# Who splits u while tiles are routed, when selections are transposed, and how many odd columns are made early in a PEER layer

## The chip, the cores and the metric

The kernel runs on one core of a Trainium2 chip. The metric is the device time of one execution in microseconds (us); several runs are given by their median. Engines carry the profile's names: PE is TensorE (matmuls), PEld its weight loads, DVE is VectorE, ACT is ScalarE, POOL is GpSimd, SP is SyncE, whose queue issues nearly all loads and stores.

## The reference, cut to what matters

The program computes two blocks on 512 tokens of width 1024; the change touches only the last layer of the second, an expert layer (PEER) with 16384 experts:

```python
def block(xb):                                   # xb: tokens x 1024
    q = (xb @ w_query).reshape(T, 8, 2, 128)     # 8 heads, 2 halves
    s = einsum('thpk,hpnk->thpn', q, sub_keys)   # 128 keys per half
    top_s, top_i = lax.top_k(s, 16)
    cand_s = top_s[:, :, 0, :, None] + top_s[:, :, 1, None, :]
    cand_i = top_i[:, :, 0, :, None] * 128 + top_i[:, :, 1, None, :]
    best_s, best_pos = lax.top_k(cand_s.reshape(T, 8, 256), 16)
    idx = take_along_axis(cand_i.reshape(T, 8, 256), best_pos, -1)
    gate = jax.nn.softmax(best_s, axis=-1)
    u, v = expert_u[idx], expert_v[idx]
    act = jax.nn.gelu(einsum('td,thkd->thk', xb, u))
    return einsum('thk,thkd->td', gate * act, v)
...
x = x + gate2 * peer(h, ...)
return rmsnorm(x, final_norm_w)
```

## The kernel before

A float32 product is made of three matmuls (`mm3`, L203): each operand is a rounded high part and a rest, and al x bh, ah x bl and ah x bh are added. The tokens are split once (`hh`, `hl`, L288, L289). A weight comes as a **unit** of 128 x 1024 values: `unit` (L190) loads 512 KB into a `raw` buffer (3 of them) through SyncE's queue, and `split` (L194) has ScalarE write `whi` (L201) and another engine the rest `wlo` (L202), VectorE unless `eng` names another. There are 8 buffers each for `whi` and `wlo`, so a unit can be split when TensorE has used the one eight before it.

The first 128 tokens take the reference's way: their selected rows of u and v are gathered by GpSimd (L1075). For the other 384 tokens the layer is computed densely. The experts are 128 columns of 128. For column j, `expert_in` (L1057) multiplies a unit of u with the tokens: 8 x 3 matmuls of 384 columns, then Gelu on ScalarE (L1063); this is called a unit of TensorE here. The 64 even columns are made early and stored in memory (`actD`), and the odd ones are made in the last stage.

`peer` runs two generators step by step. `route` first makes the queries in 16 steps (`w_q` units, L1104 onwards, with searches of the 16 best on VectorE, `top16`). Then it routes four tiles of 128 tokens, all on VectorE: candidates (`cand`, L1112), the best 16 of 256 per head, and the indices by comparing and reducing (`eq` L1137, product L1139, `si` L1142), then the softmax (`g`). `selected` (L1160) transposes `si0`, `si1` and `g` of a tile by TensorE (L1167) and copies them to `sel` on ScalarE. `gates_dense` (L1181) then makes, for 12 chunks of 32 tokens, the matrix of gates over all experts: rows `ga` and `gb` by VectorE (L1207, L1211, L1214), ScalarE or GpSimd (L1200), one matmul per token (L1217), a copy to `gst` (L1219), and four stores to memory (`gD`, L1224). Between the steps, `pace` says how many units of u are issued: its pairs are (steps, units), and they sum to 64.

`experts_out` (L1228) is the last stage. `parts(j)` (L1244) loads the gates of eight columns (`gt`, L1248), takes or makes the column's activations, multiplies them with the gates (L1258), splits the result into `wh` and `wl` (L1262, L1263), and loads and splits the unit of v. `prod` then accumulates 3 x 2 x 3 matmuls of 512 columns per column. Odd columns in `early` are made ahead of the loop:

```python
early = {j: self.expert_in(T, psp.only("pre"), j, nc.vector) for j in (1, 3, 5)}
...
ready = [parts(j) for j in range(AHEAD)]           # AHEAD = 2
```

What is written in this order is not what runs: a scheduler with a timeline of its own (`schedule_with_timeline_sim`) chooses each engine's order of instructions ahead of time, with the pools' buffers as limits. Each engine then runs its own list in order.

Of the kernel before, what the change touches and what calls it, by code (L numbers as in the profile page):

```python
# [172 lines left out]
class Block:  # L173
# [850 lines left out]
    def peer(self):  # L1024
        tc, nc, a = self.tc, self.nc, self.a
        dt = slice(128, S)
        n = S - 128
        with ExitStack() as c0:
            dr = c0.enter_context(tc.tile_pool(name="pdr", bufs=1, space=DRAM))
            self.actD = dr.tile([NSPILL, 128, n], F32, name="actD")  # L1030
            self.gD = dr.tile([12, 128, 4096], F32, name="gD")
            P = c0.enter_context(tc.tile_pool(name="pe", bufs=1, reuse_waits="tile"))
            self.acc0 = P.tile([128, D], F32, name="acc0")
            self.eid = P.tile([128, 128], I32, name="eid")
            self.gate0 = P.tile([128, 128], F32, name="gate0")
            with ExitStack() as c1:
                Q = c1.enter_context(tc.tile_pool(name="pra", bufs=1, reuse_waits="tile"))
                psp = _Banks(self.psum, t=[6, 7], u=[4, 5, 0], g=[1, 2, 3])
                sel = [Q.tile([128, NT - 1, 128], F32, name=f"sel{i}") for i in range(3)]
                iota = self.const(Q, "iota")  # L1040
                pace = [(1, 3), (15, 10), (32, 37), (24, 14)]
                self.pend = []
                work = [self.route(Q, psp, sel, iota), self.gates_dense(psp, sel, iota)]
                j, self.gpool = 0, None
                for steps, us in pace:
                    for i in range(steps):
                        _advance(work)
                        for _ in range((i + 1) * us // steps - i * us // steps):
                            act = self.expert_in(self.gpool or Q, psp, 2 * j, nc.gpsimd, "ga" if self.gpool else "act")
                            nc.sync.dma_start(self.actD[j], act)  # L1050
                            j += 1
                assert j == NSPILL
                while work:
                    _advance(work)
            self.experts_out()

    def expert_in(self, pool, psp, j, eng, tag="act"):  # L1057
        n = S - 128
        w = self.unit(self.a["p_u"][j], eng=eng)
        ps = psp.tile([128, S], F32, name="u")[:, :n]  # L1060
        self.proj_t(ps, w, self.hh, self.hl, slice(128, S))
        act = pool.tile([128, S], F32, name=tag, bufs=6)[:, :n] if tag == "ga" else pool.tile([128, n], F32, name=tag, bufs=4)
        self.nc.scalar.activation(act, ps, AF.Gelu)  # L1063
        return act

# [23 lines left out]
    def route(self, Q, psp, sel, iota):  # L1089
        tc, nc, a = self.tc, self.nc, self.a  # L1090
        with tc.tile_pool(name="rt", bufs=1, reuse_waits="tile") as R:
            sk = R.tile([128, 16, 128], F32, name="sk")
            nc.sync.dma_start(sk, a["skT"].rearrange("p (m n) -> p m n", m=16))
            val = R.tile([128, NT, 16, 16], F32, name="val")
            idx = R.tile([128, NT, 16, 16], U32, name="idx")
            for m in range(16):
                w = self.unit(a["w_q"][m])
                ps = psp.tile([128, S], F32, name="t")
                self.proj_t(ps, w, self.hh, self.hl)
                q = R.tile([128, S], F32, name="q", bufs=2)  # L1100
                nc.scalar.activation(q, ps, AF.Copy)
                ps = psp.tile([128, NT, 128], F32, name="t")
                for t in range(NT):
                    nc.tensor.matmul(ps[:, t, :], q[:, 128 * t:128 * t + 128], sk[:, m, :], start=True, stop=True)  # L1104
                sc = R.tile([128, NT, 128], F32, name="sc", bufs=2)
                nc.scalar.activation(sc, ps, AF.Copy)
                for t in range(NT):
                    self.top16(R, sc[:, t, :], val[:, t, m, :], idx[:, t, m, :])
                yield
            for t in range(NT):  # L1110
                cand = R.tile([128, 8, 16, 16], F32, name="cand")
                nc.vector.tensor_tensor(cand, val[:, t, 0::2, :, None].to_broadcast([128, 8, 16, 16]),  # L1112
                                        val[:, t, 1::2, None, :].to_broadcast([128, 8, 16, 16]), op=ALU.add)
                fi = R.tile([128, 16, 16], F32, name="fi")
                nc.vector.tensor_copy(fi, idx[:, t])
                best = R.tile([128, 8, 16], F32, name="best")
                pos = R.tile([128, 8, 16], U32, name="pos")
                yield
                for h in range(8):
                    self.top16(R, cand[:, h].rearrange("p a b -> p (a b)"), best[:, h, :], pos[:, h, :])  # L1120
                    if h == 3:
                        self.selected(psp, sel)
                    if h % 2:
                        yield
                ab = R.tile([128, 2, 8, 16], U32, name="ab")
                nc.vector.tensor_scalar(ab[:, 0], pos, 4, None, op0=ALU.logical_shift_right)
                nc.vector.tensor_scalar(ab[:, 1], pos, 15, None, op0=ALU.bitwise_and)
                abf = R.tile([128, 2, 8, 16], F32, name="abf")
                nc.vector.tensor_copy(abf, ab)
                tok = []  # L1130
                for i in range(2):
                    eq = R.tile([128, 8, 16, 16], F32, name="eq")
                    for h in range(0, 8, 4):
                        hs = slice(h, h + 4)
                        io = iota[:, None, :16].to_broadcast([128, 64, 16])
                        ab_ = abf[:, i, hs].rearrange("p h k -> p (h k)")[:, :, None].to_broadcast([128, 64, 16])
                        nc.vector.tensor_tensor(eq[:, hs].rearrange("p h k a -> p (h k) a"), ab_, io,  # L1137
                                                op=ALU.is_equal)
                    nc.vector.tensor_tensor(eq, eq, fi[:, i::2, None, :].to_broadcast([128, 8, 16, 16]),  # L1139
                                            op=ALU.mult)  # L1140
                    r = Q.tile([128, 8, 16], F32, name=f"si{i}", bufs=2)
                    nc.vector.tensor_reduce(r, eq, AX.X, ALU.add)  # L1142
                    tok.append(r)
                    yield
                g = Q.tile([128, 8, 16], F32, name="g", bufs=2)
                gs = R.tile([128, 8], F32, name="gs")
                nc.vector.tensor_tensor(g, best, best[:, :, 0:1].to_broadcast([128, 8, 16]), op=ALU.subtract)
                nc.scalar.activation(g, g, AF.Exp)
                nc.vector.tensor_reduce(gs, g, AX.X, ALU.add)
                nc.vector.reciprocal(gs, gs)  # L1150
                nc.vector.tensor_tensor(g, g, gs[:, :, None].to_broadcast([128, 8, 16]), op=ALU.mult)
                tok.append(g)
                if t == 0:
                    nc.vector.scalar_tensor_tensor(self.eid, tok[1].rearrange("p h k -> p (h k)"), 128.0,
                                                   tok[0].rearrange("p h k -> p (h k)"), op0=ALU.mult, op1=ALU.add)
                    nc.vector.tensor_copy(self.gate0, g.rearrange("p h k -> p (h k)"))
                else:
                    self.pend.append((t, [v.rearrange("p h k -> p (h k)") for v in tok]))
                yield
# [67 lines left out]
    def experts_out(self):  # L1227
# [5 lines left out]
        with ExitStack() as c0:  # L1233
# [3 lines left out]
            T = c0.enter_context(tc.tile_pool(name="eow", bufs=2, reuse_waits="tile"))  # L1237
            psp = _Banks(self.psum, u=[4, 5], pre=[0, 1, 2], acc=[0, 1, 2, 3, 6, 7])
            g2 = self.gate_row(P, psp.only("u"), 40, "g2")
            early = {j: self.expert_in(T, psp.only("pre"), j, nc.vector) for j in (1, 3, 5)}  # L1240
            acc = [[psp.tile([128, 512], F32, name="acc") for h in range(2)] for t in range(NT - 1)]
            gts = {}

            def parts(j):  # L1244
# [3 lines left out]
                    nc.sync.dma_start(gts[g].rearrange("p c j t -> p c (j t)"),  # L1248
                                      self.gD[:, :, 256 * g:256 * g + 256].rearrange("c i n -> i c n"))
                if j % 2 == 0:  # L1250
                    act = T.tile([128, n], F32, name="acts", bufs=3)
                    nc.sync.dma_start(act, self.actD[j // 2])
                elif j in early:
                    act = early.pop(j)
                else:
                    act = self.expert_in(T, psp, j, nc.vector)
                v = self.unit(a["p_v"][j])
                nc.vector.tensor_tensor(act.rearrange("p (c t) -> p c t", t=32), act.rearrange("p (c t) -> p c t", t=32),  # L1258
                                        gts[g][:, :, jj, :], op=ALU.mult)
# [107 lines left out]
```

## Time and profile before

| | us |
|---|---|
| median of 3 runs | 2299.18 (2296.61 to 2304.81) |
| profiled execution, its own time | 2295.14 |
| its span in the trace | 2293.4 |
| PE busy in the span | 2202.0 (96%) |
| DVE busy | 1653.9 (72%) |
| ACT busy | 921.4 (40%) |
| POOL busy | 817.0 (36%) |

Times of the trace count from the span's start. The queries of the layer end at about 1163 us, the tiles are routed until about 1321, the gates are made until 1472, the first product of the last stage starts at 1502, and the last matmul of the loop is near 2277. Busy shares are means over stages; what a stage waits for is read from the stretch itself. A row of the timeline gives start, duration, engine, line, operation, tiles (out<-in) and form; in square brackets stands the idle time of the engine before it and what released it.

### The profile page before, as it was taken

What the parts mean: (1) busy time and instruction counts of PE and PEld (TensorE: products, weight loads), DVE (VectorE), ACT (ScalarE), POOL (GpSimd) and SP (SyncE); (2) the same over time, 40 slices, a digit from 0 to 9 for tenths busy, and PEclk for the clock granted to TensorE, in tenths of its full rate; (3) what the DMA queues carried; (4) which work ended last, traced back from release to release, by engine and by line L of the source; (5) the groups of instructions that cost most, each with busy time, mean ns of one, the idle gap of its engine ahead of it and who ended that gap; (6) DMA issues with size and microseconds to landing.
All of it is one profiled execution on the core that took longest, in us unless ns stands there. A gap on an engine that the chain in (4) does not pass through costs nothing. (4 is left out here: it accounts for less than half of the span.)

```text
span 2293.4 us, 32152 instructions
## 1 busy us (share of the span) xinstructions
PE 2202.0 (96%) x11849; PEld 1953.9 (85%) x11849; DVE 1653.9 (72%) x3073; ACT 921.4 (40%) x1540; POOL 817.0 (36%) x611
## 2 busy tenths in 40 slices
PE   7898999999999999999998989989999999999997
PEld 6686878888889888889998989968888888888886
DVE  4346657888526478556589999678888787888888
ACT  4215544333325443343343467633333333333332
POOL 3133210000002223231456688634444443444445
PEclk9999999999999999999999999999999999999999
DMA  7423105767332321053345456799999989999996
GB/s 247 125 63 97 38 1 194 234 220 234 104 99 79 101 83 56 10 175 118 118 138 162 149 182 241 283 339 343 339 336 347 352 334 343 327 345 338 348 334 212
DMA packets 165646, 469.53 MB, mean 205 GB/s; under 512 B 18801, under 2 KB 62705, under 8 KB 165361
## 3 DMA queue, kind: packets, MB, share of 16 engines
q1 hardware_dynamic: 128624, 333.25, 42.7%
q0 software_dynamic: 36864, 134.23, 16.0%
q8 instruction: 93, 1.52, 0.3%
q14 instruction: 65, 0.52, 0.1%
HBM read 422.31 MB, written 39.85 MB: 202 GB/s over the span
## 5 line engine op out<-in xcount | busy, mean ns | idle before, releaser
L207 PE MATMUL b<-hh,wlo 128*128 128x384 f32 (+2 forms) x1872 | 657.3, 352 | 8.3 <-DVE wlo L202 2.8
L208 PE MATMUL b<-hl,whi 128*128 128x384 f32 (+2 forms) x1872 | 655.1, 350 | 3.6 <-DVE hl L289 3.4
L209 PE MATMUL b<-hh,whi 128*128 128x384 f32 (+2 forms) x1872 | 654.3, 350 | 0.0
L201 ACT ACTIVATE whi<-raw 128x1024 fp32r<-128x1024 f32 (+1 forms) x405 | 425.3, 1055 | 372.4 <-PE b L209 171.5
L202 DVE TENSOR_TENSOR wlo<-raw,whi 128x1024 fp32r<-128x1024 f32 (+1 forms) x326 | 397.7, 1228 | 201.9 <-ACT whi L201 196.6
L202 POOL TENSOR_TENSOR wlo<-raw,whi 128x1024 fp32r<-128x1024 f32 x79 | 209.2, 2661 | 527.0 <-ACT whi L201 520.4
L207 PEld LDWEIGHTS b<-hh,wlo 128*128 128x128 f32 x1872 | 354.7, 190 | 36.8 <-issue 4.3
L208 PEld LDWEIGHTS b<-hl,whi 128*128 128x128 f32 x1872 | 355.8, 190 | 30.6 <-DVE hl L289 3.8
L209 PEld LDWEIGHTS b<-hh,whi 128*128 128x128 f32 x1872 | 355.8, 190 | 25.3 <-issue 0.4
L207 PE MATMUL b<-whi,wl 128*128 128x512 f32 x768 | 299.6, 390 | 11.3 <-DVE wl L1263 11.3
L209 PE MATMUL b<-whi,wh 128*128 128x512 f32 x768 | 300.5, 391 | 0.0
L208 PE MATMUL b<-wlo,wh 128*128 128x512 f32 x768 | 300.4, 391 | 0.0
L1075 POOL DMA_INDIRECT grow<-in_p_ur_dram,eid x128 | 171.4, 1339 | 244.1 <-DVE gact L1078 170.8
L1075 POOL DMA_INDIRECT grow<-in_p_v_dram,eid x128 | 173.2, 1353 | 213.4 <-DVE acc L1080 126.7
L1063 ACT ACTIVATE act<-b 128x384 f32<-128x384 f32 x114 | 55.6, 490 | 356.1 <-PE b L209 313.5
L207 PE MATMUL b<-whi,hl 128*128 128x512 f32 (+1 forms) x464 | 179.5, 388 | 4.6 <-DVE hl L255 2.4
L207 PEld LDWEIGHTS b<-whi,wl 128*128 128x128 f32 x768 | 144.6, 188 | 40.4 <-DVE wl L1263 11.6
L209 PE MATMUL b<-whi,hh 128*128 128x512 f32 (+1 forms) x464 | 178.4, 385 | 0.0
L208 PE MATMUL b<-wlo,hh 128*128 128x512 f32 (+1 forms) x464 | 178.2, 384 | 0.0
L209 PEld LDWEIGHTS b<-whi,wh 128*128 128x128 f32 x768 | 144.5, 188 | 30.3
L208 PEld LDWEIGHTS b<-wlo,wh 128*128 128x128 f32 x768 | 144.5, 188 | 28.9
L1080 DVE SCALAR_TENSOR_TENSOR acc<-grow,gact,acc 128x1024 f32<-128x1024 f32 x127 | 162.5, 1280 | 5.8 <-DMA grow<-in_p_v_dram,eid 4.7
(296 smaller groups left out, 2972.5 us busy)
## 6 DMA issues: line engine op xcount, KB each, us to landing
raw<-in_p_u_dram SPq DMA_DIRECT2D x128, 512.0 KB, 4.5
raw<-in_p_v_dram SPq DMA_DIRECT2D x128, 512.0 KB, 6.7
raw<-in_w_adaT_dram SPq DMA_DIRECT2D x48, 512.0 KB, 3.8
gD<-gst SPq DMA_DIRECT2D x48, 512.0 KB, 4.5
gt<-gD SPq DMA_DIRECT2D x16, 1536.0 KB, 12.5
raw<-in_w_up_dram SPq DMA_DIRECT2D x44, 512.0 KB, 4.3
raw<-in_w_t_dram SPq DMA_DIRECT2D x32, 512.0 KB, 3.6
acts<-actD SPq DMA_DIRECT2D x64, 192.0 KB, 5.6
```

Of the source, the lines that this page charges most:

```text
L201: nc.scalar.activation(hi, raw, AF.Copy)
L202: (eng or nc.vector).tensor_tensor(lo, raw, hi.bitcast(F32), op=ALU.subtract)
L207: mm(out, al, bh, start=start, stop=False)
L208: mm(out, ah, bl, start=False, stop=False)
L209: mm(out, ah, bh, start=False, stop=stop)
L1063: self.nc.scalar.activation(act, ps, AF.Gelu)
L1075: nc.gpsimd.indirect_dma_start(out=g, out_offset=None, in_=rows[n], in_offset=bass.IndirectOffsetOnAxis(ap=self.eid[:, s:s + 1], axis=0))
L1080: nc.vector.scalar_tensor_tensor(self.acc0, g, act[:, s:s + 1], self.acc0, op0=ALU.mult, op1=ALU.add)
```

## The change

Three things are changed. The splits of u in the first and the third part of `pace` (37 of 64) go from GpSimd to VectorE, and three units move from the third part to the fourth. The transposes of a tile's selections are written behind the second product of the next tile instead of behind its fourth search. Five odd columns instead of three are made ahead of the last stage; for these `act` gets 6 buffers in place of 4, and `acts` 2 in place of 3.

```diff
-                pace = [(1, 3), (15, 10), (32, 37), (24, 14)]
+                pace = [(1, 3), (15, 10), (32, 34), (24, 17)]
...
-                for steps, us in pace:
+                for n_, (steps, us) in enumerate(pace):
...
-                            act = self.expert_in(self.gpool or Q, psp, 2 * j, nc.gpsimd, "ga" if self.gpool else "act")
+                            act = self.expert_in(self.gpool or Q, psp, 2 * j, nc.vector if n_ in (0, 2) else nc.gpsimd,
+                                                 "ga" if self.gpool else "act")
...
-    def expert_in(self, pool, psp, j, eng, tag="act"):
+    def expert_in(self, pool, psp, j, eng, tag="act", nact=4):
...
-        act = pool.tile([128, S], F32, name=tag, bufs=6)[:, :n] if tag == "ga" else pool.tile([128, n], F32, name=tag, bufs=4)
+        act = pool.tile([128, S], F32, name=tag, bufs=6)[:, :n] if tag == "ga" else pool.tile([128, n], F32, name=tag, bufs=nact)
...
-                    if h == 3:
-                        self.selected(psp, sel)
...
+                    if i:
+                        self.selected(psp, sel)
...
-            early = {j: self.expert_in(T, psp.only("pre"), j, nc.vector) for j in (1, 3, 5)}
+            early = {j: self.expert_in(T, psp.only("pre"), j, nc.vector, nact=6) for j in (1, 3, 5, 7, 9)}
...
-                    act = T.tile([128, n], F32, name="acts", bufs=3)
+                    act = T.tile([128, n], F32, name="acts", bufs=2)
...
-                    act = self.expert_in(T, psp, j, nc.vector)
+                    act = self.expert_in(T, psp, j, nc.vector, nact=6)
```

The scheduler makes new lists from this. Behind `L1050` the line numbers differ by one or two between the kernels. In these lists a name's number tells tiles of one name apart, and an operand without number is one of its tiles.

VectorE, second half of the routing of tile 0, before: comparisons (`eq`), products, reductions (`si`) and searches of the next tile follow each other.

```order
L1142 TENSOR_REDUCE si_9949<-eq 128x128
L1156 COPY gate_8234<-g 128x128
L1177 MATCH_REPLACE rest<-best,cand 128x256 x2
L1137 TENSOR_TENSOR eq<-abf,c_iota 128x1024 x2
L1178 MAX best<-rest 128x8 x2
L1139 TENSOR_TENSOR eq<-eq,fi 128x2048
L1179 MAX_INDEX pos<-best,rest 128x8 x2
L1142 TENSOR_REDUCE si_9989<-eq 128x128
```

The same place after:

```order
L1143 TENSOR_REDUCE si_9949<-eq 128x128
L1178 MATCH_REPLACE rest<-best,cand 128x256 x2
L202 TENSOR_TENSOR wlo<-raw,whi 128x1024
L1136 TENSOR_TENSOR eq<-abf,c_iota 128x1024 x2
L1179 MAX best<-rest 128x8 x2
L202 TENSOR_TENSOR wlo<-raw,whi 128x1024
L1138 TENSOR_TENSOR eq<-eq,fi 128x2048
L1180 MAX_INDEX pos<-best,rest 128x8 x2
L202 TENSOR_TENSOR wlo<-raw,whi 128x1024
L1143 TENSOR_REDUCE si_9989<-eq 128x128
```

Three splits stand between two reductions here, where none stood; in the whole route there are 21.

TensorE, the first matmuls of the gates (`b` is a bank of results), before:

```order
L207 MATMUL b_11576<-hh,wlo 128x384
L208 MATMUL b_11576<-hl,whi 128x384
L209 MATMUL b_11576<-hh,whi 128x384
L1217 MATMUL b_11324<-gb,ga 128x128 x4
L1217 MATMUL b_11306<-gb,ga 128x128 x4
L1217 MATMUL b_11337<-gb,ga 128x128 x4
L207 MATMUL b_11576<-hh,wlo 128x384
```

The same place after:

```order
L209 MATMUL b_11576<-hh,whi 128x384
L1168 MATMUL b_11082<-c_ident,si_10685 128x128
L1168 MATMUL b_11082<-c_ident,si_10732 128x128
L1168 MATMUL b_11082<-c_ident,g 128x128
L1168 MATMUL b_11506<-c_ident,si_11042 128x128
L1168 MATMUL b_11506<-c_ident,si_11089 128x128
L1168 MATMUL b_11506<-c_ident,g 128x128
L1218 MATMUL b_11222<-gb,ga 128x128 x4
L1218 MATMUL b_11204<-gb,ga 128x128 x4
```

The transposes of tiles 2 and 3 now stand directly ahead of the first gate matmul. Before, those of tile 2 stood among the units ahead of it, and those of tile 3 behind it.

VectorE, from the last rows of gates to the first products with `gt`, before:

```order
L1211 TENSOR_SCALAR ga_13143<-c_iota_8241,sel0_8238,sel2_8240 128x128 x4
L202 TENSOR_TENSOR wlo_13463<-raw_13460,whi_13462 128x1024
L202 TENSOR_TENSOR wlo_13500<-raw_13497,whi_13499 128x1024
L202 TENSOR_TENSOR wlo_13535<-raw_13532,whi_13534 128x1024
L1078 ISA grow_13199,gact_13198<-grow_13199,h2_6035 128x1024
L1078 ISA gact_13198 128x1
L1258 TENSOR_TENSOR act_13249<-act_13249,gt_13325 128x384
```

The same place after:

```order
L1215 TENSOR_TENSOR gb_13144<-c_iota_8241,sel1_8239 128x512
L202 TENSOR_TENSOR wlo_13422<-raw_13419,whi_13421 128x1024
L202 TENSOR_TENSOR wlo_13457<-raw_13454,whi_13456 128x1024
L202 TENSOR_TENSOR wlo_13494<-raw_13491,whi_13493 128x1024
L202 TENSOR_TENSOR wlo_13529<-raw_13526,whi_13528 128x1024
L1259 TENSOR_TENSOR act_13249<-act_13249,gt_13391 128x384
```

Four splits instead of three stand ahead of the first product with `gt`, and the gather's product (L1078) has moved behind it.

## Rows read from the trace of the kernel before

**Rows 1.** Busy time by stretch: us, PE, PEld, DVE, ACT, POOL busy (instructions), PEclk, DMA share, GB/s.

```profile
1163.00:1328.00 165.00, 147.25 (x823) 145.64 (x821) 163.91 (x367) 65.41 (x96) 106.94 (x39) 0.96 0.52 153
1328.00:1472.00 144.00, 143.84 (x1102) 143.77 (x1102) 138.19 (x360) 109.95 (x235) 120.20 (x98) 0.99 0.62 231
1472.00:1505.00 33.00, 18.89 (x88) 17.61 (x88) 14.19 (x22) 9.19 (x15) 5.78 (x6) 0.80 0.98 351
1505.00:2277.00 772.00, 772.00 (x3728) 680.32 (x3727) 630.71 (x814) 270.48 (x372) 338.52 (x250) 1.00 0.92 335
```

**Rows 2.** Waits of TensorE over the program: total us, times, longest us.

```profile
PE b L207 <- DVE wl L1263: 11.3, 1, 11.3
...
PE b L1217 <- DVE gb L1214: 6.9, 1, 6.9
...
PE b L208 <- DVE hl L289: 3.4, 2, 2.9
```

**Rows 3.** Timeline, VectorE then TensorE, ends of the route: start us, us, instruction [idle before].

```profile
1166.96 3.58 DVE L1112 TENSOR_TENSOR cand<-val 128x2048 f32<-128x2048 f32 x1
...
1321.30 5.18 DVE L1207 TENSOR_SCALAR gb<-c_iota,sel,sel 128x128 f32<-128x128 f32 x4
...
1330.26 0.86 DVE L1207 TENSOR_SCALAR gb<-c_iota,sel,sel 128x128 f32<-128x128 f32 x3
...
1328.16 1.22 PE L1217 MATMUL b<-gb,ga 128*128 128x128 f32 x4 [6.92 <-DVE gb L1214]
```

**Rows 4.** Groups by form, 1167 to 1321.3 us, VectorE then GpSimd: busy us, mean ns.

```profile
L1137 DVE TENSOR_TENSOR eq<-abf,c_iota 128x1024 f32<-128x1024 f32 x16 | 31.9, 2035 | 0.0
L1139 DVE TENSOR_TENSOR eq<-eq,fi 128x2048 f32<-128x2048 f32 x8 | 21.9, 2732 | 0.0
...
L1112 DVE TENSOR_TENSOR cand<-val 128x2048 f32<-128x2048 f32 x4 | 11.6, 2894 | 0.0
...
L1115 DVE CAST fi<-idx 128x256 f32<-128x256 uint32 x4 | 2.9, 722 | 0.0
...
L1151 DVE TENSOR_TENSOR g<-g,gs 128x128 f32<-128x128 f32 x4 | 2.5, 619 | 0.0
...
L1147 DVE TENSOR_TENSOR g<-best 128x128 f32<-128x128 f32 x4 | 2.5, 618 | 0.0
...
L1156 DVE COPY gate<-g 128x128 f32<-128x128 f32 x1 | 1.8, 1789 | 0.0
...
L202 POOL TENSOR_TENSOR wlo<-raw,whi 128x1024 fp32r<-128x1024 f32 x33 | 97.1, 2957 | 55.9 <-ACT whi L201 55.9
```

**Rows 5.** Timeline, VectorE then GpSimd: four single operations of the route and of a split.

```profile
1223.72 0.28 DVE L1115 CAST fi<-idx 128x256 f32<-128x256 uint32 x1
...
1227.80 2.27 DVE L1112 TENSOR_TENSOR cand<-val 128x2048 f32<-128x2048 f32 x1
...
1236.63 2.34 DVE L1137 TENSOR_TENSOR eq<-abf,c_iota 128x1024 f32<-128x1024 f32 x2
...
1299.27 2.40 POOL L202 TENSOR_TENSOR wlo<-raw,whi 128x1024 fp32r<-128x1024 f32 x1 [2.07 <-ACT whi L201]
```

**Rows 6.** Timeline of the hole: VectorE, then SyncE, then TensorE.

```profile
1474.57 1.30 DVE L202 TENSOR_TENSOR wlo<-raw,whi 128x1024 fp32r<-128x1024 f32 x1 [6.44 <-ACT whi L201]
1478.73 1.23 DVE L202 TENSOR_TENSOR wlo<-raw,whi 128x1024 fp32r<-128x1024 f32 x1 [2.86 <-ACT whi L201]
1483.27 1.23 DVE L202 TENSOR_TENSOR wlo<-raw,whi 128x1024 fp32r<-128x1024 f32 x1 [3.31 <-ACT whi L201]
1484.41 1.22 DVE L1078 CUSTOM_DVE_ANT_0 grow<-grow,h 128x1024 f32<-128x1024 f32 x1
...
1495.70 1.50 DVE L1258 TENSOR_TENSOR act<-act,gt 128x384 f32<-128x384 f32 x3 [10.07 <-DMA gt<-gD]
...
1482.02 0.49 SPq L1248 DMA_DIRECT2D gt<-gD  x1
...
1501.87 0.79 PE L207 MATMUL b<-whi,wl 128*128 128x512 f32 x1 [11.32 <-DVE wl L1263]
```

## The prediction

> **What bounds the kernel now.** I read the stretches first. In the last stage (1505 to 2277 us) TensorE is busy 772.00 us of 772.00, and in the gate stage (1328 to 1472 us) 143.84 of 144.00 [rows 1]. There only work taken off TensorE shortens the time. Time without work is left in two places that the change touches. While tiles are routed (1163 to 1328 us) TensorE works 147.25 us of 165.00 and VectorE 163.91: VectorE sets the end. In the hole before the first product (1472 to 1505 us) TensorE works 18.89 of 33.00 at a granted clock of 0.80, with the DMA engines at 0.98 [rows 1]. The list of waits then says who ends the idle time: 11.3 us at the first product for the weights of v's gates (L1263), 6.9 us at the first gate matmul for gb (L1214), and 2.9 us at most for hl when the stage starts [rows 2].
>
> VectorE's route runs without a gap from the first cand at 1166.96 to the first gate rows at 1321.30, which is 154.3 us; the first gate matmul starts at 1328.16 [rows 3]. Part of this is not VectorE's own work. Its two-operand operations take longer while GpSimd splits: the sixteen eq take 31.9 us, the eight products 21.9, the four cand 11.6, and small copies up to 1.8 each, beside 33 splits on GpSimd [rows 4]. Undisturbed, a pair of eq takes 2.34, a cand or a product (both 2048 wide) 2.27, a small copy 0.28 [rows 5]. The excess is 31.9 - 8 x 2.34 = 13.2; 21.9 - 8 x 2.27 = 3.7; 11.6 - 4 x 2.27 = 2.5; and 1.8 + 1.4 + 1.4 + 1.5 for the four small groups: 25.5 us, or 0.78 per split of GpSimd. Searches with one operand show none.
>
> **The change, part by part.** All sums are against the profiled execution's 2295.14 us.
>
> *Splits on VectorE.* Of the units of u, 37 get their subtraction from VectorE. In VectorE's order 21 stand between the first cand and the last reduction of the route, and one more just ahead of it. A split on VectorE delays the next instruction by 1.14 us (1483.27 to 1484.41) [rows 6], so this adds 21 x 1.14 = 23.9, and 1.14 ahead of it. It removes the 33 splits of GpSimd from that stretch and with them the 25.5. So this half of the change is near to nothing: VectorE pays in work what it paid in waiting. But the third segment ends before the route does. GpSimd's order holds 11 splits of the fourth segment that start as soon as a buffer is freed, and these fall beside the second half of the route. At the rate above they cost 11 x 0.78 = 8.6. Nearest bounds: nothing, if they meet one-operand searches; and the whole length of an undisturbed split, 2.40 [rows 5], each: 26.4. I take the rate because it is a mean over 33 of them in the same program. I add 2.3 (0 to 6) for the first gate rows that GpSimd builds in the same stretch and for splits that wait for whi. Behind the route VectorE's first four gate rows no longer meet GpSimd: 5.18 us before, while three of the same alone take 0.86 [rows 3], so four 1.1: -4.1. When the stage starts, three splits go to VectorE ahead of hl: between -2.9 (the wait is gone [rows 2]) and +3.4 (three splits in front); I take +1.0.
>
> *Selections a tile later.* Before, tile 3's transposes stood behind the first gate matmuls in TensorE's order. Now tile 2's and tile 3's six transposes all stand ahead of the first one. So short waits become one long one. TensorE has 32.4 units ahead of the first gate matmul (before 33.9). A unit takes 4.16 us of TensorE, as the splits at 1474.57 and 1478.73 show, each released by the end of one unit [rows 6]. 32.4 x 4.16 = 134.8 from 1163: it is done at about 1298, and then waits for VectorE some 35 us. The first gate matmul is VectorE's to give, and all terms so far move it one for one: 1.0 + 1.1 - 25.5 + 23.9 + 8.6 + 2.3 - 4.1 = **+7.3 us**, to about 1335.5.
>
> *Work carried into the gate stage.* Between the first and the last gate matmul TensorE now has 338 matmuls of units, before 314, and three transposes fewer: 24 x 4.16 / 24 = 4.2, less an estimated 0.4 for the transposes (the 128 wide matmuls at 0.1 each): **+3.8**. Nothing hides it, since this stage has no idle time.
>
> *Five odd columns.* After the last gate matmul TensorE had 3 units and 7 matmuls ahead of the first product, 13.7 us; now it has 4 units and 22 matmuls, 20.5 us. The product itself hangs on the last gates' way through memory: the load of gt is issued at 1482.02, about 10 us after the last gate matmul (1472, where the stretch of [rows 1] ends), lands by 1495.70, and the product starts at 1501.87 [rows 6]. In the new order SyncE's queue has one raw load ahead of gt instead of two, but four splits of VectorE precede its first product with gt instead of three. I take this chain as 29.6 us against 29.9: **-0.3**. So the added 6.8 us lie in the hole's idle time, and one unit less is left for the last stage: **-4.2**. That is the one sure gain. Two more columns made early do not mean two units less, since one of the two moves work that already stood ahead of the first product. The act and acts buffers change nothing that a row shows: cost nothing, while loads land before use.
>
> Sum: 7.3 + 3.8 - 0.3 - 4.2 = **+6.6**. 2295.14 + 6.6 = 2301.7 own time. The median of the runs is 2299.18, 4.0 above the profiled execution, so **2305.7**. A measurement can tell about 0.3%, 6.9 us, from no change, so this lies at the very bound.
>
> **A rule against the change.** The rows show VectorE's pair of eq at 2.34 undisturbed and at 31.9/8 = 4.0 in the mean beside GpSimd [rows 4, 5]. The Trainium skill, "SBUF — State Buffer", section "Who interferes with whom", says that VectorE's second port and GpSimd's are one shared pair, held as an exclusive lock. By that rule in its strict form every split left on GpSimd would shut out the route's two-operand work for its whole length, which is the third case below. The rate of 0.78 of 2.40 agrees with the lock for a third of the time, about the share of such operations in the route (46 of 129 us undisturbed).
>
> **Rivals.** *The late splits fall into gaps.* The 11 meet searches and the start gains: then 8.6 and 2.3 fall away, the start gives up to -2.9, and if gt also lands some us earlier, since fewer loads share the queue, the hole's remaining 9 us shrink. Sum: from 6.6 - 8.6 - 2.3 - 3.9 = -8, and to -14 with gt, up to +2. For it: the new route's waits for whi could pull the two apart. Against it: GpSimd starts whenever a buffer comes free, and two-operand work is over a third of VectorE's time. It ends faster than before where the 11 cost under 0.18 us each. This is the case on the other side.
> *Each late split blocks for its whole length.* 11 x 2.4 in place of 8.6: up to +24, from +13. For it: the worst pair of eq are far above the mean. Against it: 33 splits cost 25.5 together, not 79.
> *The hole is not shortened.* If gt is late by the 4.2 us, or the unit made early is paid by a later hole, the last term is gone: about +11. For it: DMA share 0.98 there [rows 1]. Against it: the chain starts from the last gate matmul as before.
>
> **Chances.** Forecast (+2 to +13) 0.55: of it 0.29 within 6.9 us and 0.26 slower. Late splits in gaps 0.24: 0.12 faster, 0.12 within. Full blocking 0.13 and no shorter hole 0.08, both slower. So faster 0.12, the same 0.41, slower 0.47. Range: from -5 to +18.5 about the median, 2294 to 2318, which leaves out the lower part of the first rival and the top of the second. The forecast's own range is 2301 to 2312.
>
> **What would show it.** In the new trace: VectorE without idle time until about 1333; pairs of eq at 2.34 until the fourth segment's splits begin on GpSimd near 1256, and longer ones behind that; in the list of waits one wait of some 35 us of TensorE ahead of the first gate matmul in place of several short ones; the first gate matmul near 1335.5 and the last near 1483; idle time of about 9 us before the first product near 1513; and 768 us to the tail with TensorE always busy. I am wrong if eq stays long although GpSimd is quiet (then it is not GpSimd that stretches it), if the first gate matmul comes before 1328, or if TensorE shows idle time in the last stage.

## The result, and the profile after

The changed kernel takes **2319.27 us** (median of 6 runs, 2316.48 to 2320.29), the kernel before 2296.70 beside it (6 runs): a ratio of 1.0092, 95% interval 1.0074 to 1.0109. On the scale of the prediction, whose median before was 2299.18, that is 2320.3: slower, as forecast, but by 21 us and not by 6.6, and just above the range's top of 2318 (the two medians themselves are 22.6 apart). Its profiled execution has a span of 2315.8 us, 22.4 more than before.

Where the 22.4 us lie is read best by cutting both traces at the same five events: the last matmul of the scores, the first and the last matmul of the gates, the first product (the first L207 of `whi` and `wl` behind them), and TensorE's last matmul.

| us, from the traces | before | after | difference | forecast |
|---|---|---|---|---|
| to the last scores | 1163.0 | 1165.2 | +2.2 | +1.0 |
| to the first gate matmul | 165.2 | 169.4 | +4.2 | +6.3 |
| gates, first to last matmul | 144.1 | 153.7 | +9.6 | +3.8 |
| hole, to the first product | 29.6 | 27.8 | -1.8 | -0.3 |
| last stage, to TensorE's last matmul | 777.7 | 773.5 | -4.2 | -4.2 |
| tail, to the end | 13.8 | 26.2 | +12.4 | 0 |

The first difference is not the change's alone: the scores end at 1161.8 us in one and at 1174.8 in another of the kernels below (e1, e2). The stretches of the changed kernel between these events, with the columns of [rows 1]:

```profile
1165.20:1334.60 169.40, 138.01 (x789) 136.01 (x788) 167.68 (x390) 62.28 (x93) 41.58 (x15) 0.91 0.44 143
1334.60:1488.30 153.70, 151.06 (x1123) 150.33 (x1124) 140.66 (x359) 113.78 (x239) 120.28 (x100) 0.98 0.60 221
1488.30:1516.10 27.80, 20.46 (x118) 20.14 (x117) 10.50 (x16) 9.85 (x17) 4.62 (x5) 0.94 1.01 366
1516.10:2289.60 773.50, 773.47 (x3720) 680.46 (x3720) 630.29 (x819) 266.06 (x371) 342.57 (x250) 1.00 0.93 335
2289.60:2315.80 26.20, 0.03 (x1) 0.00 (x0) 14.46 (x19) 5.12 (x16) 11.12 (x13) 0.59 0.30 110
```

The kernel before at the same events, gates, last stage and tail:

```profile
1328.20:1472.20 144.00, 144.00 (x1102) 143.93 (x1103) 138.00 (x359) 109.95 (x235) 120.27 (x99) 0.99 0.62 231
...
1501.90:2279.60 777.70, 777.64 (x3744) 684.54 (x3744) 636.40 (x824) 270.48 (x372) 342.14 (x253) 1.00 0.92 334
2279.60:2293.40 13.80, 0.00 (x0) 0.00 (x0) 8.70 (x13) 5.12 (x16) 6.79 (x10) 0.64 0.39 152
```

TensorE is busy without a gap in the last stage and has 24 matmuls less there (3720; before 3744), as forecast. But the gate stage, 144.00 of 144.00 before, now has 2.6 us without work, and behind TensorE's last matmul 26.2 us follow in which VectorE is busy for more than half.

The list of waits of TensorE, with the columns of [rows 2]:

```profile
PE b L1168 <- DVE si L1143: 29.4, 4, 11.3
...
PE b L207 <- DVE wl L1264: 7.4, 1, 7.4
...
PE b L1218 <- POOL ga L1201: 2.6, 3, 1.4
```

The wait for `gb` ahead of the first gate matmul (6.9 [rows 2]) has become waits for the last reductions, and a new kind has come up: gate matmuls that wait for rows that GpSimd builds. In the timeline of TensorE the long wait comes in pieces, one for each transpose of `si`:

```profile
1312.36 0.45 PE L1168 MATMUL b<-c_ident,si 128*128 128x128 f32 x1 [9.85 <-DVE si L1143]
...
1324.91 0.47 PE L1168 MATMUL b<-c_ident,si 128*128 128x128 f32 x1 [11.26 <-DVE si L1143]
...
1332.04 0.45 PE L1168 MATMUL b<-c_ident,si 128*128 128x128 f32 x1 [6.66 <-DVE si L1143]
...
1334.60 2.72 PE L1218 MATMUL b<-gb,ga 128*128 128x128 f32 x11 [1.27 <-DVE gb L1215]
```

The first gate matmul starts at 1334.60, before at 1328.16 [rows 3]. The route's price can be read in VectorE's groups, first from 1168 to 1260 us, where GpSimd does nothing, then from 1260 to 1334 us, beside its eleven late splits:

```profile
L1136 DVE TENSOR_TENSOR eq<-abf,c_iota 128x1024 f32<-128x1024 f32 x6 | 7.2, 1279 | 0.0
L1138 DVE TENSOR_TENSOR eq<-eq,fi 128x2048 f32<-128x2048 f32 x3 | 7.1, 2353 | 0.0
```

```profile
L1136 DVE TENSOR_TENSOR eq<-abf,c_iota 128x1024 f32<-128x1024 f32 x10 | 15.3, 1574 | 0.0
L1138 DVE TENSOR_TENSOR eq<-eq,fi 128x2048 f32<-128x2048 f32 x6 | 15.3, 2548 | 0.0
...
L1116 DVE CAST fi<-idx 128x256 f32<-128x256 uint32 x2 | 2.1, 1071 | 0.0
```

An `eq` takes 1279 ns with GpSimd quiet and 1574 beside it; before, over the whole route, 2035 [rows 4]. So the forecast that GpSimd's splits stretch VectorE's two-operand work, and that the stretch goes where they go, holds.

The tail is read in VectorE's timeline. TensorE's last matmul starts at 2289.24, and behind it VectorE still adds gathered rows (`acc`, L1081) between the operations on the last tiles (L1278, L1279):

```profile
2289.35 1.28 DVE L1279 TENSOR_TENSOR x<-x,b 128x512 f32<-128x512 f32 x2
2290.54 0.70 DVE L1278 TENSOR_TENSOR b<-b,g 128x512 f32<-128x512 f32 x1
2291.14 0.68 DVE L1279 TENSOR_TENSOR x<-x,b 128x512 f32<-128x512 f32 x1
2291.74 1.28 DVE L1081 SCALAR_TENSOR_TENSOR acc<-grow,gact,acc 128x1024 f32<-128x1024 f32 x1
2292.93 0.70 DVE L1278 TENSOR_TENSOR b<-b,g 128x512 f32<-128x512 f32 x1
2293.53 0.69 DVE L1279 TENSOR_TENSOR x<-x,b 128x512 f32<-128x512 f32 x1
2294.12 1.29 DVE L1081 SCALAR_TENSOR_TENSOR acc<-grow,gact,acc 128x1024 f32<-128x1024 f32 x1
2295.32 0.69 DVE L1279 TENSOR_TENSOR x<-x,b 128x512 f32<-128x512 f32 x1
2295.92 2.60 DVE L1081 SCALAR_TENSOR_TENSOR acc<-grow,gact,acc 128x1024 f32<-128x1024 f32 x2
```

The same rows of the kernel before, its last accumulation and what GpSimd makes of it for the first tile; the last line is GpSimd's in the changed kernel:

```profile
2274.67 1.28 DVE L1080 SCALAR_TENSOR_TENSOR acc<-grow,gact,acc 128x1024 f32<-128x1024 f32 x1 [1.00 <-DMA grow<-in_p_v_dram,eid]
...
2276.10 2.55 POOL L1277 TENSOR_TENSOR acc<-acc,g 128x512 f32<-128x512 f32 x2 [5.58 <-DVE acc L1080]
...
2298.68 2.48 POOL L1278 TENSOR_TENSOR acc<-acc,g 128x512 f32<-128x512 f32 x2 [8.04 <-DVE acc L1081]
```

Before, the last accumulation ends at 2275.95, 3.6 us before TensorE does (2279.55); now it ends at 2298.52, 8.9 us behind it (2289.63). From it to the end it is 17.4 us before (2293.37) and 17.3 after (2315.84): two operations on GpSimd, a norm, a scaling, a store. So the end of both programs follows the gather's last row, which moved by 22.6 us, and not TensorE, which moved by 10.1.

### The profile page after: what moved, and what is told of

Its sections match the earlier page's. It is cut to its first block, busy times and chain, and to the rows that moved or that the text cites. A ratio compares the mean times of both kernels' runs of the same rounds, so it can differ in the third digit from the quotient of the medians.

```text
span 2315.8 us, 32112 instructions
## 1 busy us (share of the span) xinstructions
PE 2201.4 (95%) x11849; PEld 1953.1 (84%) x11849; DVE 1672.7 (72%) x3110; ACT 918.0 (40%) x1540; POOL 720.8 (31%) x574
## 3 DMA queue, kind: packets, MB, share of 16 engines
q0 software_dynamic: 36864, 134.23, 16.1%
## 5 line engine op out<-in xcount | busy, mean ns | idle before, releaser
L207 PE MATMUL b<-hh,wlo 128*128 128x384 f32 (+2 forms) x1872 | 655.4, 351 | 0.8 <-DVE cy L1008 0.6
L202 DVE TENSOR_TENSOR wlo<-raw,whi 128x1024 fp32r<-128x1024 f32 (+1 forms) x363 | 441.4, 1223 | 224.8 <-ACT whi L201 219.6
L207 PEld LDWEIGHTS b<-hh,wlo 128*128 128x128 f32 x1872 | 354.1, 190 | 27.7 <-DVE cy L1008 0.8
L207 PE MATMUL b<-whi,wl 128*128 128x512 f32 x768 | 299.6, 390 | 7.4 <-DVE wl L1264 7.4
L202 POOL TENSOR_TENSOR wlo<-raw,whi 128x1024 fp32r<-128x1024 f32 x42 | 110.0, 2629 | 598.8 <-ACT whi L201 598.8
L1076 POOL DMA_INDIRECT grow<-in_p_ur_dram,eid x128 | 180.5, 1410 | 235.5 <-DVE gact L1079 177.1
L207 PE MATMUL b<-whi,hl 128*128 128x512 f32 (+1 forms) x464 | 179.7, 388 | 4.5 <-DVE hl L255 2.4
L207 PEld LDWEIGHTS b<-whi,wl 128*128 128x128 f32 x768 | 144.6, 188 | 36.5 <-DVE wl L1264 7.7
L1081 DVE SCALAR_TENSOR_TENSOR acc<-grow,gact,acc 128x1024 f32<-128x1024 f32 x127 | 163.1, 1284 | 3.3 <-DMA grow<-in_p_v_dram,eid 2.3
```

The costliest lines, as they stand in the source:

```text
L202: (eng or nc.vector).tensor_tensor(lo, raw, hi.bitcast(F32), op=ALU.subtract)
L207: mm(out, al, bh, start=start, stop=False)
L1076: nc.gpsimd.indirect_dma_start(out=g, out_offset=None, in_=rows[n], in_offset=bass.IndirectOffsetOnAxis(ap=self.eid[:, s:s + 1], axis=0))
L1081: nc.vector.scalar_tensor_tensor(self.acc0, g, act[:, s:s + 1], self.acc0, op0=ALU.mult, op1=ALU.add)
```

## The experiments

The theory from the trace (A): the route and the gate stage are later as above, and the tail is made by the gather's place in VectorE's list. The rivals: the later transposes are the cause; the tail belongs to the last tiles or to the five columns; the gate stage's loss is GpSimd's speed.

### One part of the change at a time

Only the transposes (e1), the splits with the new pace and the transposes (e2), only the five columns (e3), and the splits alone with the pace of before (e4):

```diff
-                    if h == 3:
-                        self.selected(psp, sel)
...
+                    if i:
+                        self.selected(psp, sel)
```

is e1; e2 is this, and

```diff
-                pace = [(1, 3), (15, 10), (32, 37), (24, 14)]
+                pace = [(1, 3), (15, 10), (32, 34), (24, 17)]
...
-nc.gpsimd
+nc.vector if n_ in (0, 2) else nc.gpsimd
```

while e4 is the last two of these lines alone; in both, the loop over `pace` counts its parts as `n_`, as in the change. e3 is

```diff
-            early = {j: self.expert_in(T, psp.only("pre"), j, nc.vector) for j in (1, 3, 5)}
+            early = {j: self.expert_in(T, psp.only("pre"), j, nc.vector, nact=6) for j in (1, 3, 5, 7, 9)}
...
-                    act = T.tile([128, n], F32, name="acts", bufs=3)
+                    act = T.tile([128, n], F32, name="acts", bufs=2)
```

with the 6 buffers for `act` of the change.

> Only the selections are transposed a tile later; splits, pace and early columns as before. Theory A (the later transposes are no cause: VectorE sets the end of the route and its list is the same): within 3 us of the kernel before. Theory B (six transposes ahead of the first gate matmul are what moves it): the first gate matmul 5 to 7 us later and the time up by as much.

> Splits of u on VectorE with the new pace, and the later transposes, but three odd columns as before. Theory A (the gather's accumulations have slipped behind the last tiles' work in VectorE's list, and this comes with the splits): first gate matmul near 1335, last near 1488, TensorE's last matmul near 2294, and the end 20 us or more behind it, so 17 to 22 us slower than before. Theory B (the tail of the changed kernel comes from the five odd columns alone): the end 14 us behind TensorE's last matmul, so 13 to 16 us slower.

> Only five odd columns are made early; splits, pace and transposes as before. The prediction's step (a unit of TensorE taken into the hole): 4 to 5 us faster. Theory A (the gather's last accumulations stand later in VectorE's list, one of them behind the first product of the last bank, and the end hangs on them): TensorE's last matmul 4 to 6 us earlier, but the time 0 to 5 us above that of before.

> Splits of u on VectorE, but 37 units in the third segment of the pace as before (24 splits in the route, no more units in the gate stage than before), three odd columns, transposes written as before. Theory A: route 9 to 11 us longer than before, gate stage as long as before without the wait for ga, last accumulation 4 to 6 us later against TensorE's end than before: 10 to 15 us slower. Theory B (the whole loss is in the gate stage and the tail of the five columns): within 5 us of before.

The kernel before had a median of 2299.44 in these runs. The stages as above, in us:

| | median | ratio (95%) | scores to first gate | gates | hole | last stage | tail |
|---|---|---|---|---|---|---|---|
| e1 | 2296.53 | 0.9993 (0.9982 to 1.0005) | 164.6 | 144.4 | 29.2 | 778.0 | 13.4 |
| e2 | 2323.73 | 1.0103 (1.0075 to 1.0131) | 169.4 | 153.8 | 25.6 | 778.8 | 24.5 |
| e3 | 2301.28 | 1.0008 (0.9996 to 1.0020) | 167.3 | 144.9 | 29.8 | 773.8 | 20.8 |
| e4 | 2304.40 | 1.0026 (1.0016 to 1.0035) | 175.8 | 139.4 | 28.4 | 778.2 | 14.8 |

The later transposes do nothing by themselves. That all six stand ahead of the first gate matmul comes with the splits on VectorE: e4 has them there too, with the transposes written as before.

The five columns give what was forecast and lose it again: TensorE's last stage is 3.9 us shorter, the tail 7.0 longer. The timeline of VectorE in e3 shows how:

```profile
2281.45 0.67 DVE L1278 TENSOR_TENSOR x<-x,b 128x512 f32<-128x512 f32 x1
2282.04 0.69 DVE L1277 TENSOR_TENSOR b<-b,g 128x512 f32<-128x512 f32 x1
2282.64 1.27 DVE L1080 SCALAR_TENSOR_TENSOR acc<-grow,gact,acc 128x1024 f32<-128x1024 f32 x1
2283.83 1.27 DVE L1278 TENSOR_TENSOR x<-x,b 128x512 f32<-128x512 f32 x2
2291.44 2.74 DVE L1282 SCALAR_TENSOR_TENSOR x<-x,r,fw 128x512 f32<-128x512 f32 x4 [6.33 <-POOL r L237]
```

The last accumulation stands behind an operation on the last bank, and the first scaling then waits 6.33 us for the first tile's norm. In VectorE's list the gather's rows lie between the splits, about 16 rows to 12 splits, and the splits go at TensorE's pace. At the 242nd operation of the gather (the second accumulation of its last head) 3 splits are left in the list of before, 2 in e3 and e4, 1 in e2 and in the changed kernel. e3 and e4 stand alike there, but TensorE ends 3.9 us earlier in e3, and its last accumulation comes 3.4 us behind TensorE's last matmul, in e4 2.6 us before it. A unit less for TensorE thus brings nothing while the gather keeps its place.

e2 carries nearly the whole loss, also the tail of 24.5: theory B (a tail of the five columns alone) falls. e2 is 24 us slower than the kernel before, where theory A had 17 to 22. Its profiled execution is longer than its median tells, since the scores end 9 us later in it than in the changed kernel; the stages behind it do not depend on that.

e4 is 10 to 15 us slower by my expectation and 5 us by the runs, the upper edge of its theory B. From the scores to the first gate matmul it is 6.4 us longer than e2 (three splits more, at 1.14, are 3.4 of it), but the gate stage is 14.4 us shorter, and the tail only 1.0 longer than before. So the splits as such do not make most of the loss: 1.0103 against 1.0026, with intervals apart. e2 has two things more than e4, the three units moved from the third part of the pace to the fourth and the later transposes. The transposes do nothing beside splits on GpSimd (e1), so I take the three units for the cause; without the transposes they were not run.

### The tail

The last head's gathers left out, 32 of 256 rows, in the changed kernel (e5) and in the one before (e6):

```diff
-        for h in range(8):
+        for h in range(7):
             hs = slice(16 * h, 16 * h + 16)
```

> The changed kernel without the gather's last head: 32 of the 256 gathered rows, and with them a part of the first 128 tokens' sum, are left out. Theory A (the end hangs on the gather's last accumulations in VectorE's list): the end 12 to 15 us behind TensorE's last matmul instead of 26, so 11 to 14 us below the changed kernel's time, near 2306. Theory B (the tail belongs to the last tiles' own work): as long as the changed kernel.

> The kernel before without the gather's last head (the same part left out). Theory A: only what of the gather was still at the end before goes, 0 to 3 us faster. If the gather itself slowed the last stage by what it loads or by VectorE's time, it would be 10 us or more faster.

Medians 2300.43 and 2290.43, the kernel before 2296.27 beside them: ratios 1.0021 (1.0011 to 1.0030) and 0.9968 (0.9955 to 0.9982). The tail is 8.0 us in both, and their last stages are as long as with all rows (773.4 and 778.2). So the end of the gather, with the order of the last operations that comes with it, is worth 26.2 - 8.0 = 18.2 us of the changed kernel's tail and 5.8 of the tail before. I had expected 11 to 14 and 0 to 3: I took the tail of before for the last tiles' own work, and part of it was the gather already. Theory B is excluded. What the change loses without the gather's end is the rest, 2300.43 against 2290.43: 10 us.

Can the gather be moved ahead without leaving anything out? With a fifth buffer for its rows throughout (e8, kernel before):

```diff
-GROWS = 4
+GROWS = 5
...
-                    act = T.tile([128, n], F32, name="acts", bufs=3)
+                    act = T.tile([128, n], F32, name="acts", bufs=2)
```

> The kernel before with five buffers for gathered rows instead of four, and two for acts instead of three, for the room. Theory A: all accumulations of the gather stand ahead of the last splits in VectorE's list, and the end goes down by what the gather held in the tail before, 0 to 4 us. Rival (a faster gather takes DMA time from v): slower by 2 us or more.

It is 2356.12 us, ratio 1.0279 (1.0245 to 1.0313): slower, as the rival had it, and by far more than 2 us. The tail is 8.1 us, but the last stage 833.7. The waits of TensorE over the program (the longest of the first kind is the hole's):

```profile
PE b L207 <- DVE wl L1263: 41.2, 16, 11.0
...
PE b L207 <- DVE wlo L202: 11.1, 7, 2.8
```

and the waits of VectorE from 1510 to 2330 us:

```profile
DVE wlo L202 <- ACT whi L201: 43.7, 42, 3.6
DVE acts L1258 <- DMA acts<-actD: 28.1, 10, 8.7
```

The loads of `acts` come late (before, 2.7 us in 4 waits of the same kind), but they do not explain TensorE's waits: 15.8 of the 28.1 us lie behind 2230 us, after the last of them (2212), and the three waits ahead of that come 13 us and more before TensorE's next one. What stands directly ahead of a wait of TensorE is shown by ScalarE and TensorE near 1990 us:

```profile
1988.08 0.49 ACT L1063 ACTIVATE act<-b 128x384 f32<-128x384 f32 x1 [5.73 <-PE b L209]
...
1990.88 0.50 PE L207 MATMUL b<-whi,wl 128*128 128x512 f32 x1 [2.84 <-DVE wl L1263]
```

TensorE ends a unit of u at 1988.04, and the next in its list is a product that needs this unit: it waits 2.84 us for Gelu, the product with the gates and the split. Before, 36 matmuls of products stand between any two units from 1600 to 1900 us, and TensorE never waits there; in e8 there are between 1 and 71. Seven of the waits in the last stage are of this kind (2.79 to 2.84 us each, 19.7 together), half of its 38.5 us without work. Seven others, 9.1 us together, come behind a unit of v for whose load ScalarE, and then VectorE with `wlo`, had waited: these have the rival's reason. The granted clock is at half for 28.4 us of the stage, before for 3.3, which adds some 12. So the new buffers changed the scheduler's list, and its order makes half of the time without work. Two buffers for `acts` alone do not do this: the changed kernel has them, and TensorE does not wait in its last stage.

So only for the end: a fifth buffer for every fifth row of the last two heads, in the changed kernel (e9) and with five columns alone (e10), and for the last head alone in the kernel before (e11):

```diff
-                    g = P.tile([128, D], F32, name="grow", bufs=GROWS)
+                    g = P.tile([128, D], F32, name="growx", bufs=1) if h >= 6 and s % 5 == 4 else P.tile([128, D], F32, name="grow", bufs=GROWS)
...
-        last = 4
+        last = 3
```

(e11: `h == 7`, `last` as before, `acts` with 2 buffers.)

> The changed kernel with a fifth buffer for every fifth gathered row of the last two heads, and three instead of four columns in the last pass, for the room. In VectorE's list all accumulations now stand ahead of the last tiles' work; nothing is left out. Theory A (the place of the accumulations makes the tail): the end 8 to 11 us behind TensorE's last matmul instead of 26, 12 to 18 us below the changed kernel. Rival (what a faster gather takes from v's loads, some 10 us per 100 us with five buffers throughout, comes back as waits of TensorE): TensorE's last matmul 5 to 15 us later, and less than half of the gain left.

> The kernel before with five early columns and the same fifth buffer in the last two heads and three columns in the last pass; splits, pace and transposes as before. Theory A: TensorE's last matmul 4 us earlier than before, the end 8 to 11 us behind it instead of 14: 6 to 10 us faster than before, which no other kernel here is. Rival (loads of v late): no faster than before.

> The kernel before with a fifth buffer for every fifth gathered row of the last head only, and two buffers for acts instead of three. Theory A: the end 8 to 11 us behind TensorE's last matmul, 2 to 6 us faster than before. Rival: no change.

| | median | ratio (95%) | last stage | tail |
|---|---|---|---|---|
| e9 | 2314.55 | 1.0086 (1.0060 to 1.0113) | 780.7 | 12.8 |
| e10 | 2295.44 | 1.0001 (0.9990 to 1.0011) | 777.7 | 12.8 |
| e11 | 2299.25 | 1.0012 (0.9996 to 1.0028) | 777.6 | 13.2 |

The kernel before had 2295.74 in these runs. In e9 the tail shrinks by 13.4 us, so the place of the accumulations does make it; but TensorE's last matmul comes 7.2 us later against the first product, and the time is 4.7 us below the changed kernel's instead of 12 to 18, with overlapping intervals. TensorE's waits there, from 1520 to 2300 us:

```profile
PE b L207 <- DVE wl L1264: 2.8, 1, 2.8
PE b L207 <- DVE wlo L202: 1.9, 3, 1.4
```

Two thirds of the 7.2 us are these waits. The other 2.5 us are longer busy time for as many matmuls; the granted clock is at half (0.5, the level of 1.2 GHz) for 5.8 us of the stage, in the changed kernel for 3.5, which explains about half of them. In e10, too, 3.9 us of the unit come back in the last stage, and the tail is 12.8, not 8, though the last accumulation ends at 2268.98 there, 11 us before TensorE does. What keeps that tail long can be read from VectorE's first operation on a finished bank, in e10 and in e6:

```profile
2276.77 0.70 DVE L1277 TENSOR_TENSOR b<-b,g 128x512 f32<-128x512 f32 x1 [1.87 <-PE b L209]
```

```profile
2268.88 1.38 DVE L1277 TENSOR_TENSOR b<-b,g 128x512 f32<-128x512 f32 x2 [5.29 <-PE b L209]
```

From it to the end it is 16 to 17 us in both (16.1 and 16.8). But e10 gets the first bank 3.4 us before TensorE's last matmul ends, as e9 and e11 do, and e6 8.8 us before it, as e5 and e8 do. So behind the gather stands the order in which TensorE finishes its banks; no run changes that order alone. None of these is faster than the kernel before, so I have no version to offer that beats both.

### The gate stage

Seven buffers for `ga` in the changed kernel (e7):

```diff
-                    A = G.tile([128, S], F32, name="ga", bufs=6).rearrange("p (a b) -> p a b", a=4)
+                    A = G.tile([128, S], F32, name="ga", bufs=7).rearrange("p (a b) -> p a b", a=4)
```

(the same in `expert_in`, whose activations take their buffers from the same set).

> The changed kernel with seven buffers for ga instead of six. Theory A (GpSimd's gate rows wait at 1428 us for a buffer whose activation is stored late, since the store stands behind loads of raw in SyncE's queue): the 2.6 us of waits for ga and the half clock behind them go, 4 to 6 us below the changed kernel. Rival (GpSimd itself is too slow with the six splits left to it): no change.

2314.96 us, ratio 1.0084 (1.0057 to 1.0110), 4.3 below the changed kernel's median; the intervals of the two overlap. Its trace speaks more clearly: the gate stage takes 148.3 instead of 153.7 us, and of TensorE's waits in it only the first one, for `gb`, is left. The timelines of GpSimd and then of SyncE in the changed kernel show where the wait came from:

```profile
1428.27 8.97 POOL L1201 TENSOR_SCALAR ga<-c_iota,sel,sel 128x128 f32<-128x128 f32 x8 [7.01 <-DMA actD<-ga]
```

```profile
1417.35 6.52 SPq L193 DMA_DIRECT2D raw<-in_p_u_dram  x2
1423.96 0.38 SPq L1051 DMA_DIRECT2D actD<-ga  x1
```

GpSimd stood idle for 7.01 us until the store of an activation gave its buffer free. That store was issued at 1423.96, behind two loads of `raw` in the same queue, which took 6.52 us to issue. The activation that it stores was made from 1421.07 to 1421.55:

```profile
1421.07 0.48 ACT L1064 ACTIVATE ga<-b 128x384 f32<-128x384 f32 x1
```

So 2.4 us of the wait lie between the activation and the store's issue, the queue's part at most, and 4.3 us between the issue and GpSimd's start. e7 shows what one buffer more is worth, not what another queue would be.

### The price of a split on GpSimd

The fourth segment's splits on VectorE too (e12):

```diff
-nc.vector if n_ in (0, 2) else nc.gpsimd
+nc.vector if n_ in (0, 2, 3) else nc.gpsimd
```

> The changed kernel with the splits of the fourth segment on VectorE too: 32 splits in the route instead of 21, none on GpSimd beside it. At the forecast's price the route gets 11 x 1.14 = 12.5 us of work and loses the some 8 us of waiting that the changed kernel's trace shows: the first gate matmul 4 to 5 us later, the time 2 to 6 us above the changed kernel's. If a split on GpSimd shut out two-operand work for its whole length (26 us for 11), the first gate matmul would be 14 us earlier; if it cost nothing, 12.5 us later.

2319.87 us, ratio 1.0092 (1.0075 to 1.0109): as long as the changed kernel, where 2 to 6 us more were expected. From the scores to the first gate matmul it takes 176.2 us, 6.8 more than the changed kernel, where 4 to 5 were expected: 11 splits on VectorE cost 12.5 and give 12.5 - 6.8 = 5.7 us of waiting back, 0.52 for each split on GpSimd. That is neither nothing nor the whole 2.40. The gate stage is 147.4 us, 6.3 shorter, and pays for it.

## Why the prediction was right, and by how much it was not

**Slower** was right, and the route was its largest term. The direction does not hang on the tail: the other stages add up to 10.0 us (7.8 without the stretch up to the scores), and e5 is 10.0 us slower than e6. "About 1335.5" for the first gate matmul was 1334.60, partly by luck. The route's first `cand` came at 1170.30, 3.3 us later than before, where 2.1 were forecast; from it to the first gate rows VectorE took 161.5 us, 7.2 more than before, where 9.3 were forecast; the first gate rows gave their 4.1. The removed 25.5 us of waiting and the added 23.9 us of splits cancel, and the eleven late splits cost 8 us together with GpSimd's first gate rows: in the groups above, the ten `eq` are 15.3 - 5 x 2.34 = 3.6 over, the six products 15.3 - 6 x 2.27 = 1.7, the two casts 2.1 - 2 x 0.28 = 1.5, and one small `g` (1.69 us, at 1282) another 1.4. The terms were 8.6 and 2.3. e12 gives the late splits by themselves 5.7. The Trainium skill, "SBUF — State Buffer", section "Who interferes with whom", would have a held pair shut out the other engine for a whole instruction. The price of 0.52 to 0.78 per split of 2.40 us means that this meets a split for less than a third of its time here. So the third case was too dear.

**The later transposes** got no term in the sum except 0.4 us for their matmuls, and by themselves they change nothing (e1). That six transposes stand ahead of the gates was read rightly, but it follows from the splits. The one long wait of some 35 us came as several, 29.4 us in 4 for `si`.

**The gate stage** was mis-sized: "+3.8. Nothing hides it, since this stage has no idle time". The 24 matmuls are there, and 5.4 us more (e7). They came from a buffer that I had not looked at: the units moved into this stage put their activations into the buffers of GpSimd's gate rows, and these are freed by stores in SyncE's queue. The prediction did not follow these buffers through the gate stage. With the pace of before the stage is 139.4 us (e4).

**The hole and the unit** came out as forecast: -1.8 for -0.3 and -4.2 for -4.2.

**The step that failed** is the end of the sum: "768 us to the tail with TensorE always busy". The sum stops at TensorE's last matmul and takes the tail as fixed. TensorE was always busy, and the tail grew by 12.4 us, more than half of the loss. The profile of before had shown that the end hung on the gather as well as on TensorE: the last accumulation ended 3.6 us before TensorE's last matmul, and the order of the new kernel, which the prediction read around the gates and around `gt`, has six accumulations behind the first operation on the last tiles at the end of VectorE's list, four of them behind TensorE's last matmul; the list of before has one. So "that is the one sure gain" was not sure: e3 gains it on TensorE and loses it in the tail.

Of the rivals, the late splits in gaps and the full blocking did not happen, and the hole was shortened. The mechanism that decided was in none of them.

## What to carry to other kernels

When two chains end within a few microseconds of each other, a saving on one is worth only what the other leaves, and a delay of either is paid in full: find every chain that reaches the last store, and read the order of the new kernel there first. A chain that is woven into another engine's list by position moves with that list, so count how many of its steps stand behind the last work of the bound engine. Where a step is moved into another stage, follow the buffers it shares there and the queue that frees them. And where a scheduler makes the lists, a buffer more can change the order of every engine (e8): read the new list before the loss is put down to the transfers.

## What the runs showed of the hardware that was not expected

VectorE's recorded durations can grow without costing time. In the changed kernel the searches of 256 values take 0.52 us each at 1228 us and 0.42 at 1282, but from one search to the next it is 0.40 us in both places:

```profile
1227.86 0.52 DVE L1180 FIND_INDEX8 pos<-best,rest 128x8 uint32<-128x256 f32 x1
...
1228.26 0.52 DVE L1180 FIND_INDEX8 pos<-best,rest 128x8 uint32<-128x256 f32 x1
...
1281.78 0.42 DVE L1180 FIND_INDEX8 pos<-best,rest 128x8 uint32<-128x256 f32 x1
...
1282.18 0.42 DVE L1180 FIND_INDEX8 pos<-best,rest 128x8 uint32<-128x256 f32 x1
```

The growth is gradual, from 0.45 us at 1177 us to 0.52 at 1228, and gone at 1236. Sums over a route are better made from start to start.

With a fifth buffer for gathered rows and two for `acts` (e8) the last stage took 56 us more (833.7 against 777.7), while the share of the DMA engines rose only from 0.92 [rows 1] to 0.95 (1505 to 2100 us). Of TensorE's 38.5 us without work there, 9.1 stand behind late loads of v and 19.7 behind the order of its own list, so the 56 us are not the price of so high a share.
